# A planner that credits VectorE for TensorE's side products, and other costs in its ledger, in a two-layer decoder step

## The chip, the core and the metric

One NeuronCore of a Trainium2 chip runs the whole program. The metric is the time of one execution on the device, in microseconds; the comparison is between medians of repeated runs. Five engines matter: TensorE (PE in the profile; PEld is its loading of stationary operands), VectorE (DVE), ScalarE (ACT), GpSimd (POOL) and SyncE (SP), whose queue issues most of the transfers. Each runs its own instructions in the order in which the program gives them, and waits for the others by semaphores.

## What is computed

One inference step of a decoder with two layers, for 256 prompt tokens and 8 sequences of 4 tokens (288 columns in all), width 1024, in float32. In each layer four token mixers run beside each other on one input projection, and their outputs are merged through sigmoid gates:

```python
g_cols, u_pool, u_conf, u_sc, q, k, v, qi, ki, wi = split_cols(x @ w_in)
a_out, new_pool = pool_mixer(u_pool, ...)
cv, new_conf = causal_dwconv(ga * jax.nn.sigmoid(gb), st_conf, conv_w)       # 31 taps, 256 channels
b_out = jax.nn.silu(layer_norm(cv + conv_b, conv_ln_g, conv_ln_b))
c_out = sb * cc                                                              # short convolution, 3 taps
d_out = attend(q, k, v, qi, ki, wi)                                          # top-k by indexer scores, then softmax
merged = gates[0]*(a_out @ w_br_pool) + gates[1]*(b_out @ w_br_conv) + gates[2]*(c_out @ w_br_sconv) + gates[3]*(d_out @ w_br_attn)
x1 = layer_norm(ALPHA * x + merged @ w_o, ln1_g, ln1_b)
r = ALPHA * x1 + (silu(hg) * hu) @ w_ffn_out
r = r + (pe @ w_pe) * jax.nn.sigmoid(r @ w_pg)
y = layer_norm(r, ln2_g, ln2_b)
```

## The kernel before

**Weights.** All weights are 128x128 tiles, 2448 of them, in groups of eight (`G`). A group is loaded by one transfer on SP's queue (`load`, L252), ScalarE rounds it to its high half (`high`, L260, tile `whi`), and VectorE makes the low half as the difference (`low`, L267, tile `wlo`). Inputs are split in the same way, and `mm3` (L289) multiplies each tile three times, high by high, high by low and low by high, in three matmuls of 288 columns (L292 to L294; L318 to L324 where several outputs grow together). A group is thus 24 matmuls. `fetch` (L237) issues transfers five groups ahead of the matmuls, high halves three and low halves two ahead; `wlo` has three buffers.

**Order.** The order is written out by the program, engine by engine, and a planner fills it. `W` (L277) is called for each tile; at the first tile of a group it calls `fetch` and then `side` (L205). `side` is one tick of the planner: it raises `left`, what remains of VectorE's and ScalarE's time in this group, by `budget` = (1.96, 2.3) us, with no surplus carried over but debts kept, and then steps the tasks that are awake, as long as `left` is above zero for the engines that a task needs. A task is a generator; it issues instructions and yields their cost (VectorE, ScalarE), or a number of ticks to sleep. So what a task issues in a tick stands, on every engine, behind the weight halves that `fetch` has just issued and ahead of the group's 24 matmuls; that holds for the tasks' own TensorE work too (the "products": index scores, attention scores, transposes, convolution statistics). Work outside the tasks, the evacuation of projections, is issued behind its group and takes its cost off with `cost` (L219). `finish` (L223) steps tasks to their end without ticks of weight work between.

**Tasks.** In each layer `layer` (L1110) starts the 31-tap convolution `conv` (L670) at the lowest rank, `index_prompt` (L756), `index_sample` (L928), `attn_prompt` (L801), `attn_sample` (L970), `sconv` (L568) and `pool` (L603). They run beside the projections: q, k, v with rotary, short convolution, pool, gates 0 and 2, branches 0 and 2, gates 1 and 3. Then the attention tasks are finished, branch 3 runs, the convolution is finished, and w_o with branch 1 begins. A convolution step is one `scalar_tensor_tensor` on 128x256 (L684, planned at 0.49).

**Banks.** Projections rotate through four PSUM banks (`mm`), products through four (`ax`, `get_ax`). A projection of 8 row blocks fills one bank in a group. A branch (`branch`, L1067) of `nk` = 2 row blocks fills four in a group; VectorE multiplies each by its gate (L1075 for the first branch; L1078, then an addition on GpSimd at L1079), and 0.37 is charged behind each.

**Last norm.** `ln` (L386) ends by `first` (VectorE multiplies by the inverse deviation, L439) and `second` (scale and shift). In the last norm (`not after`) ScalarE does `second` (L446) for all channel blocks but 3 and 7, which VectorE does (L448); six transfers of the output (L453) follow on SP.

## Time and profile before

| | us |
|---|---|
| median of three runs | 1073.88 (1073.39 to 1074.95) |
| the profiled execution | 1073.4 |
| its span on the core | 1071.5 |
| TensorE's matmuls busy | 1055.5 |
| VectorE busy | 763.2 |
| ScalarE busy | 564.2 |
| GpSimd busy | 157.1 |

The span is from the first to the last instruction of the program; 1.9 us of the profiled execution's time lie around it. A matmul's record is longer than the distance to the next matmul, since matmuls are pipelined: whether TensorE loses time is read from the distance between starts and from its idle time, not from busy time alone. Layer 0's mixers lie at about 28 to 245 us, layer 1's at about 557 to 777; between and behind them are w_o, feed-forward, gate projection and norms. `[idle <-X]` behind an instruction says how long its engine stood idle before it, and what ended that.

### The profile page before, as it was taken

What the parts mean: (1) busy time and instruction counts of PE and PEld (TensorE: products, weight loads), DVE (VectorE), ACT (ScalarE), POOL (GpSimd) and SP (SyncE); (2) the same over time, 40 slices, a digit from 0 to 9 for tenths busy, and PEclk for the clock granted to TensorE, in tenths of its full rate; (3) what the DMA queues carried; (4) which work ended last, traced back from release to release, by engine and by line L of the source; (5) the groups of instructions that cost most, each with busy time, mean ns of one, the idle gap of its engine ahead of it and who ended that gap; (6) DMA issues with size and microseconds to landing.
All of it is one profiled execution on the core that took longest, in us unless ns stands there. A gap on an engine that the chain in (4) does not pass through costs nothing.

```text
span 1071.5 us, 20583 instructions
## 1 busy us (share of the span) xinstructions
PE 1055.5 (98%) x8078; PEld 1022.4 (95%) x8078; DVE 763.2 (71%) x1319; ACT 564.2 (53%) x950; POOL 157.1 (15%) x177
## 2 busy tenths in 40 slices
PE   9999999999999999999999999999999999999996
PEld 8999989899999999999999999898999999999996
DVE  5898869668785565544789888786688756555456
ACT  4886446554564444434578665554645644443344
POOL 0530003005500000000425100030055000000004
PEclk9999999999999999999999999999999999999998
DMA  8577646554455555544555766465453545554541
GB/s 304 168 247 213 201 144 227 197 167 147 150 164 172 157 171 168 174 157 169 161 183 164 264 190 216 122 225 205 139 169 128 186 158 170 171 171 159 171 143 45
DMA packets 61778, 188.57 MB, mean 176 GB/s; under 512 B 7602, under 2 KB 12274, under 8 KB 61682
## 3 DMA queue, kind: packets, MB, share of 16 engines
q1 hardware_dynamic: 60546, 183.55, 52.8%
q0 software_dynamic: 992, 3.57, 1.0%
q8 instruction: 63, 1.03, 0.4%
q14 instruction: 33, 0.27, 0.1%
q10 hardware_dynamic: 144, 0.15, 0.1%
HBM read 182.49 MB, written 4.75 MB: 175 GB/s over the span
## 4 chain that ended last, share of the span: by engine, by line
PE 90%; DVE 4%; ACT 2%; issue 1%; DMA 1%; POOL 1%; SPq 1%; POOLq 0%; DVEq 0%; ACTq 0%
PE mm L292 25%; PE mm L293 25%; PE mm L294 24%; PE mm L322 2%; PE mm L324 2%; PE mm L318 2%; DVE wlo L271 1%; DMA wraw<-in_w_dram 1%; POOL b L374 1%; PE ax L293 1%; PE ax L294 1%; PE ax L292 1%; DVE b L684 1%; PE ax L993 1%; PE ax L1030 1%
## 5 line engine op out<-in xcount | busy, mean ns | idle before, releaser
L271 DVE TENSOR_TENSOR wlo<-wraw,whi 128x1024 fp32r<-128x1024 f32 (+1 forms) x309 | 385.7, 1251 | 161.6 <-issue 80.8
L292 PE MATMUL mm<-xh,whi 128*128 128x288 f32 x1536 | 455.5, 297 | 1.0 <-DVE s L1078 1.0
L293 PE MATMUL mm<-xl,whi 128*128 128x288 f32 x1536 | 453.1, 295 | 0.0
L294 PE MATMUL mm<-xh,wlo 128*128 128x288 f32 x1536 | 452.9, 295 | 0.2 <-DVE wlo L271 0.2
L264 ACT ACTIVATE whi<-wraw 128x1024 fp32r<-128x1024 f32 (+1 forms) x309 | 322.7, 1047 | 160.8 <-PE mm L293 80.7
L292 PEld LDWEIGHTS mm<-xh,whi 128*128 128x128 f32 x1536 | 288.8, 188 | 9.3 <-issue 7.3
L294 PEld LDWEIGHTS mm<-xh,wlo 128*128 128x128 f32 x1536 | 288.6, 188 | 0.6 <-DVE wlo L271 0.6
L293 PEld LDWEIGHTS mm<-xl,whi 128*128 128x128 f32 x1536 | 288.8, 188 | 0.3
L292 PE MATMUL mm<-b,whi 128*128 128x288 f32 x576 | 171.5, 298 | 1.9 <-DVE m L1075 1.9
L293 PE MATMUL mm<-b,whi 128*128 128x288 f32 x576 | 169.9, 295 | 0.0
L294 PE MATMUL mm<-b,wlo 128*128 128x288 f32 x576 | 169.5, 294 | 0.0
L292 PEld LDWEIGHTS mm<-b,whi 128*128 128x128 f32 x576 | 107.9, 187 | 2.8 <-DVE m L1075 2.6
L294 PEld LDWEIGHTS mm<-b,wlo 128*128 128x128 f32 x576 | 108.5, 188 | 0.0
L293 PEld LDWEIGHTS mm<-b,whi 128*128 128x128 f32 x576 | 108.1, 188 | 0.2
L1079 POOL TENSOR_TENSOR m<-m,s 128x288 f32<-128x288 f32 x32 | 37.7, 1209 | 268.5 <-DVE s L1078 268.5
L343 POOL TENSOR_TENSOR b<-xf 128x288 f32<-128x288 f32 x4 | 4.9, 1215 | 443.0 <-DVE xf L1230 434.4
L1203 ACT ACTIVATE b<-s 128x288 fp32r<-128x288 f32 x44 | 19.2, 444 | 92.3 <-DVE s L1198 92.3
L684 DVE SCALAR_TENSOR_TENSOR b<-b,prm 128x256 f32<-128x256 f32 x120 | 58.9, 539 | 0.1
L1198 DVE TENSOR_TENSOR s<-s,mm 128x288 f32<-128x288 f32 x40 | 18.0, 454 | 50.6 <-PE mm L294 50.6
L1063 ACT ACTIVATE xf<-mm 128x288 f32<-128x288 f32 x32 | 13.2, 411 | 53.9 <-PE mm L294 53.8
L1063 ACT ACTIVATE g<-mm 128x288 f32<-128x288 f32 x32 | 13.2, 411 | 47.9 <-PE mm L294 47.8
L1206 DVE TENSOR_TENSOR b<-s,b 128x288 fp32r<-128x288 f32 x44 | 19.8, 457 | 19.4 <-ACT b L1203 19.4
(252 smaller groups left out, 1198.2 us busy)
## 6 DMA issues: line engine op xcount, KB each, us to landing
wraw<-in_w_dram SPq DMA_DIRECT2D x304, 512.0 KB, 3.5
kv<-in_ck_dram SPq DMA_DIRECT2D x32, 260.0 KB, 5.3
kv<-in_cv_dram SPq DMA_DIRECT2D x32, 256.0 KB, 5.2
out_ko_dram<-b POOLq DMA_DIRECT2D x2, 576.0 KB, 3.4
out_vo_dram<-b POOLq DMA_DIRECT2D x2, 576.0 KB, 5.8
kv<-in_kidx_dram SPq DMA_DIRECT2D x32, 32.0 KB, 2.8
b<-in_p_dram SPq DMA_DIRECT2D x3, 288.0 KB, 3.8
wraw<-in_w_dram SPq DMA_DIRECT2D x3, 256.0 KB, 5.3
```

What stands on the lines that cost most here:

```text
L264: self.nc.scalar.activation(self.hi[g][:, c[i]], self.raw[g][:, c[i]], AF.Copy)
L271: self.nc.vector.tensor_tensor(self.lo[g][:, c[i]], self.raw[g][:, c[i]], self.hi[g][:, c[i]].bitcast(F32), op=OP.subtract)
L292: m(out, wh, rh, start=first, stop=False)
L293: m(out, wh, rl, start=False, stop=False)
L294: m(out, wl, rh, start=False, stop=last)
L318: m(o, wh, rh[:, k], start=k == 0, stop=False)
L322: m(o, wh, rl[:, k], start=False, stop=not early and k == nk - 1)
L324: m(o, wl, rh[:, k], start=False, stop=False)
L684: nc.vector.scalar_tensor_tensor(o, e, wj, o, op0=OP.mult, op1=OP.add)
L1063: self.nc.scalar.activation(g, a, AF.Sigmoid)
L1079: nc.gpsimd.tensor_tensor(self.m[:, j], self.m[:, j], t, op=OP.add)
L1206: nc.vector.tensor_tensor(h[:, 1, i % 2], t, h[:, 0, i % 2].bitcast(F32), op=OP.subtract)
```

## The change

- `budget` for ScalarE is 2.1 instead of 2.3; a gate is charged 0.41 instead of 0.3; the exponentials of `attn_prompt` are issued only in a tick where ScalarE has 1.6 left.
- A new `gain` adds 0.8 of a product's time to what is left of VectorE's budget, at the places where products are issued.
- Three sleeps of one tick become two, ahead of the convolution's mean, the normalised transposes and the sample's index product, and one of two becomes three, ahead of the prompt's index products.
- The convolution's mean and variance are one matmul each, of a sum that VectorE makes first, instead of two; the two squares are made by VectorE instead of ScalarE.
- `branch` charges 0.46 for an evacuation instead of 0.37, and those of the first group before its first tile; each evacuation later charges for one of the group to come.
- In the last norm GpSimd scales block 6 and ScalarE block 3.

```diff
@@ -129,7 +129,7 @@
-        self.budget = (1.96, 2.3)
+        self.budget = (1.96, 2.1)
@@ -219,6 +219,10 @@
         self.left[1] -= a
+
+    def gain(self, t):
+
+        self.left[0] += 0.8 * t
@@ -442,7 +446,9 @@
             y = ys.pop(k)
-            if not after and k not in (3, 7):
+            if not after and k == 6:
+                nc.gpsimd.tensor_scalar(xf[:, k], y, g[:, k:k + 1], b[:, k:k + 1], op0=OP.mult, op1=OP.add)
+            elif not after and k < KD - 1:
                 nc.scalar.activation(xf[:, k], y, AF.Identity, bias=b[:, k:k + 1], scale=g[:, k:k + 1])
@@ -694,24 +700,29 @@
             nc.vector.tensor_scalar(cv[:, c, TP:], cv[:, c, TP:], bias[:, c:c + 1], None, op0=OP.add)
             yield 0.1, 0
+        both = self.s()
+        nc.vector.tensor_tensor(both, cv[:, 0], cv[:, 1], op=OP.add)
+        yield 0.45, 0
         yield BOTH
         self.free()
         self.free()
-        yield 1
+        yield 2
         mu, var = yield from self.get_ax(2)
         mu, var = mu[:, :N], var[:, :N]
-        for c in range(2):
-            nc.tensor.matmul(mu, self.c("o1024"), cv[:, c], start=c == 0, stop=c == 1)
+        nc.tensor.matmul(mu, self.c("o1024"), both, start=True, stop=True)
+        self.gain(0.25)
         sq = [self.s(), self.s()]
         for c in range(2):
             nc.vector.scalar_tensor_tensor(cv[:, c], mu, -4.0, cv[:, c], op0=OP.mult, op1=OP.add)
             yield 0.4, 0
         for c in range(2):
-            nc.scalar.activation(sq[c], cv[:, c], AF.Square)
-        yield 0, 0.8
+            nc.vector.tensor_tensor(sq[c], cv[:, c], cv[:, c], op=OP.mult)
+            yield 0.45, 0
+        nc.vector.tensor_tensor(sq[0], sq[0], sq[1], op=OP.add)
+        yield 0.45, 0
         yield 1
-        for c in range(2):
-            nc.tensor.matmul(var, self.c("o1024"), sq[c], start=c == 0, stop=c == 1)
+        nc.tensor.matmul(var, self.c("o1024"), sq[0], start=True, stop=True)
+        self.gain(0.25)
         sd = self.s()
         nc.scalar.activation(sd, var, AF.Sqrt, bias=self.c("eps"), scale=4.0)
         yield 0, 2.0
@@ -758,7 +769,7 @@
         yield 0, 0.33
-        yield 2
+        yield 3
         wp = self.sb.tile([128, 2, 4], F32, name="wp", tag="wp", bufs=1)
@@ -776,6 +787,7 @@
                                  start=True, stop=True)
+            self.gain(0.4 + n / 400)
             for e in range(2):
@@ -833,6 +846,7 @@
                                      self.k[r, h // 2, :n], start=True, stop=True)
+                self.gain(1.1)
@@ -846,6 +860,8 @@
             yield 1
+            while self.left[1] < 1.6:
+                yield 1
             for h in range(8):
@@ -857,7 +873,7 @@
                 yield 0.06 + n / 1920, 0
-            yield 1
+            yield 2
             pts = []
@@ -881,6 +898,7 @@
                                          pts[kc][:, 2 * c + s], start=kc == 0, stop=kc == i)
+            self.gain(1.0 * (i + 1))
             self.free(len(pts))
@@ -939,12 +957,13 @@
             yield 0, 0.22
-        yield 1
+        yield 2
         a = yield from self.get_ax()
         for p in range(4):
             nc.tensor.matmul(a[32 * p:32 * p + 32, :NK], self.qibd[:, p].rearrange("p r h t -> p (r h t)"),
                              self.kx[:, p], start=True, stop=True)
         nc.tensor.matmul(a[:, 288:288 + NS], self.c("hsel")[:4], self.wi[:, TP:], start=True, stop=True)
+        self.gain(1.2)
         rl = self.sb.tile([128, NK], F32, name="rls", tag="rls", bufs=1)
@@ -993,6 +1013,7 @@
                                      kt[j][:, :, c], start=False, stop=c == 3)
+            self.gain(2.3)
@@ -1029,6 +1050,7 @@
                                      start=False, stop=kc == 1)
+            self.gain(3.0)
@@ -1061,16 +1084,19 @@
             g = self.xf[:, j] if spare else self.sb.tile([128, N], F32, name="g", tag="g", bufs=9)
             self.nc.scalar.activation(g, a, AF.Sigmoid)
-            self.cost(0, 0.3)
+            self.cost(0, 0.41)
             self.gates[i, j] = g
 
     def branch(self, i, name, nk, first=False):
         nc = self.nc
         h, l = self.br.pop(name)
+        now = G // nk
+        self.cost(0.46 * now, 0)
         for j in range(KD):
             a, = self.proj("w_br_" + name, [128 * j], h, l, nk)
             g = self.gates.pop((i, j))
-            self.cost(0.37, 0)
+            if j + now < KD:
+                self.cost(0.46, 0)
             if first:
...
```

Further calls of `gain`, each behind its product: 0.4 behind a transposition of v, 0.35 behind four transposes of the probabilities and of the sample's output, 0.6 behind the sample's index sum.

## Rows read from the trace of the kernel before

**Rows 1.** Page of the profile, parts 1 and 4: busy time; last chain by engine.

```profile
PE 1055.5 (98%) x8078; PEld 1022.4 (95%) x8078; DVE 763.2 (71%) x1319; ACT 564.2 (53%) x950; POOL 157.1 (15%) x177
...
PE 90%; DVE 4%; ACT 2%; issue 1%; DMA 1%; POOL 1%; SPq 1%; POOLq 0%; DVEq 0%; ACTq 0%
```

**Rows 2.** Windows view: stretch; us, busy us (instructions) by engine, clock, DMA share, GB/s.

```profile
44.00:77.00 33.00, 33.00 (x252) 32.29 (x251) 31.27 (x67) 27.46 (x57) 12.31 (x15) 1.00 0.67 213
```

**Rows 3.** Timeline, TensorE, 38 to 46: start, us, line, operation, tiles, count, [idle <-releaser].

```profile
41.65 0.29 PE L294 MATMUL mm<-xh,wlo 128*128 128x288 f32 x1
...
43.61 0.71 PE L777 MATMUL ax<-ki,qi 64*128 64x128 f32 x6 [1.03 <-ACT ki L759]
44.25 0.40 PE L292 MATMUL mm<-xh,whi 128*128 128x288 f32 x1
```

**Rows 4.** Timeline, VectorE, 162 to 180, layer 0's branches.

```profile
163.57 1.23 DVE L271 TENSOR_TENSOR wlo<-wraw,whi 128x1024 fp32r<-128x1024 f32 x1 [0.30 <-issue]
164.71 1.67 DVE L684 SCALAR_TENSOR_TENSOR b<-b,prm 128x256 f32<-128x256 f32 x4
166.41 1.55 DVE L1075 TENSOR_TENSOR m<-mm,xf 128x288 f32<-128x288 f32 x4
...
174.22 1.73 DVE L271 TENSOR_TENSOR wlo<-wraw,whi 128x1024 fp32r<-128x1024 f32 x1
...
176.83 1.54 DVE L1078 TENSOR_TENSOR s<-mm,g 128x288 f32<-128x288 f32 x4
```

**Rows 5.** Waits, 160 to 180: who waited for whom, us, times, longest.

```profile
PE mm L292 <- DVE s L1078: 0.6, 1, 0.6
...
PE mm L292 <- DVE m L1075: 0.3, 1, 0.3
```

**Rows 6.** Waits, 690 to 712, layer 1's branches.

```profile
PE mm L292 <- DVE m L1075: 1.7, 2, 0.9
...
PE mm L292 <- DVE s L1078: 0.3, 1, 0.3
```

**Rows 7.** Timeline, ScalarE, 688 to 712.

```profile
691.72 1.28 ACT L851 ACT_TABLE_LOAD   x1
...
698.37 0.41 ACT L1063 ACTIVATE g<-mm 128x288 f32<-128x288 f32 x1
```

**Rows 8.** Chain that ended last, in order of time: start, us, what.

```profile
222.64 0.97 PE ax L704 x4
226.79 0.97 PE ax L714 x4
```

**Rows 9.** Groups by line, VectorE, shapes apart: busy us, mean ns | idle before.

```profile
L736 DVE TENSOR_TENSOR b<-b,s 128x288 f32<-128x288 f32 x4 | 1.6, 452 | 0.0
```

**Rows 10.** Timeline, TensorE, 573 to 574.6, the same products in layer 1.

```profile
573.16 0.29 PE L294 MATMUL mm<-xh,wlo 128*128 128x288 f32 x1
...
574.25 0.40 PE L292 MATMUL mm<-xh,whi 128*128 128x288 f32 x1
```

**Rows 11.** Timeline, VectorE, 690 to 712.

```profile
699.76 1.23 DVE L271 TENSOR_TENSOR wlo<-wraw,whi 128x1024 fp32r<-128x1024 f32 x1 [1.39 <-ACT whi L264]
```

**Rows 12.** Windows view of instructions on the ax banks alone.

```profile
77.00:162.00 85.00, 14.43 (x130) 8.06 (x130) 6.62 (x14) 6.40 (x16) 1.00 0.61 196
```

**Rows 13.** Windows view, all instructions.

```profile
77.00:162.00 85.00, 85.00 (x663) 78.38 (x663) 68.73 (x157) 45.95 (x93) 1.50 (x3) 1.00 0.61 196
```

**Rows 14.** Timeline, GpSimd, 1057 to 1072.

```profile
1062.69 3.80 POOL L434 TENSOR_TENSOR xf<-xf,b 128x288 f32<-128x288 f32 x5 [2.34 <-ACT b L419]
```

**Rows 15.** Timeline, SP's queue, 1057 to 1072.

```profile
1065.29 3.76 SPq L453 DMA_DIRECT2D out_y_dram<-xf  x6
```

**Rows 16.** Timeline, VectorE, 1057 to 1072.

```profile
1065.98 0.67 DVE L448 TENSOR_SCALAR xf<-s,prm 128x288 f32<-128x288 f32 x1
...
1067.78 0.43 DVE L448 TENSOR_SCALAR xf<-s,prm 128x288 f32<-128x288 f32 x1
```

**Rows 17.** Timeline, VectorE, 28 to 46.

```profile
35.24 1.97 DVE L684 SCALAR_TENSOR_TENSOR b<-b,prm 128x256 f32<-128x256 f32 x2
```

More of the change, by code (lines that the diff above doesn't have):

```diff
@@ L811, in attn_prompt @@
                 nc.tensor.transpose(a[:rows, 128 * c:128 * (c + 1)], self.v[:, c, 128 * i:128 * i + rows], ident)
+            self.gain(0.4)
             nc.scalar.activation(vt[:, i] if i < 2 else vs, a[:rows], AF.Copy)
@@ L871, in attn_prompt @@
                                                              128 * kc:128 * (kc + 1)], ident)
+                    self.gain(0.35)
                     nc.scalar.activation(pt[:, h0:h0 + 4], v, AF.Copy)
@@ L957, in index_sample @@
         nc.tensor.matmul(a[:NS, :NK], ws, rl, start=True, stop=True)
+        self.gain(0.6)
         sc = self.sb.tile([NS, NK], F32, name="scs", tag="scs", bufs=1)
@@ L1040, in attn_sample @@
             self.free()
+            self.gain(0.35)
             w = slice(TP + 16 * f, TP + 16 * f + 16)
```

## The prediction

> **What bounds the kernel now.** I read the page's shares first: TensorE's matmuls are busy for 1055.5 of 1071.5 us, and the chain that ended last lies on TensorE for 90% of the span [rows 1]. So there are two ways to gain: less work on TensorE, or fewer of the 16 us in which it stands still. VectorE and ScalarE cost nothing by being busy; they cost where TensorE waits for them. I therefore went along TensorE's timeline and the chain of waits, looking for gaps between one weight matmul and the next. In the stretch 44 to 77 us 252 matmuls take 33.00 us [rows 2], a step of 0.13 us. Against that step three kinds of gap stand in the stages that the change touches: a product in layer 0 that waits for its operand [rows 3], evacuations that come late where branches follow each other [rows 4 to 7], and the products themselves, which are work and stay. The part between the layers' attention stages (feed-forward, layer norms) is not touched but for the last norm.
>
> **The change part by part.**
>
> *Two products become one, in four places.* The convolution's mean and variance take two matmuls each; the pair takes 0.97 us of the chain, for the mean as for the variance [rows 8], so one takes 0.485. Two pairs in each of two layers: 4 x 0.485 = **1.94 us** off TensorE. In their place VectorE gets, per layer, one sum ahead of the mean, two squares (from ScalarE) and one sum of squares: four operations of the kind that takes 0.45 [rows 9], 1.8 us. This lies at the end of the convolution, a chain that nobody awaits until after the fourth branch, so I cost it at nothing. If that cover is gone, it is because the variance product, which still stands one group behind its operand, comes up before five VectorE operations in a row are through (2.3 us behind the mean, of a group's 3.2); then the whole group of weight matmuls queues behind it on TensorE, and the square root waits for it. That is up to 0.5 us in each layer, and stands in the term for new waits.
>
> *The index product one group later.* In layer 0 the key copy on ScalarE comes late and the first index products stand 1.03 us idle for it: from the last weight matmul before them to the first one behind them go 41.65 to 44.25, 2.60 us [rows 3]. The same products in layer 1 take 573.16 to 574.25, 1.09 us [rows 10]. The difference, 1.51 us, is wait. A group is 24 matmuls, 3.2 us, so one group more removes the wait. What is late next is VectorE: in 44 to 77 it is busy for 31.27 of 33.00 us [rows 2], 1.73 us free, and the change gives it there 0.8 x (0.72 + 1.04) = 1.4 us of budget (the two credits of the index products, worked out from the code). TensorE would arrive 1.5 us sooner at an engine with no more room than that; only the low halves that were made ahead give a little. Bounds 0.3 and 1.5; I take **0.9 us**. The other products that move by a group (transposes, sample index, convolution) show no such idle time, so they gain nothing; the attention chain gets up to three groups longer by them, and the page loads that it issues on SP between the weight loads move along, at no cost as long as the chain ends within the last gates.
>
> *The branches.* A branch of two row blocks has four outputs in a group and four banks, so an output's evacuation must be through within one group. Before, the cost (0.37) is taken off only behind each output: the planner fills the first group with convolution steps and then finds that it is short. One sees this at 163.57: low half, four convolution steps (1.67), and only at 166.41 the first evacuation [rows 4]; again at 174.22 with a step between low half and evacuation at 176.83. TensorE stands idle 0.3 + 0.6 us in layer 0 [rows 5] and 1.7 + 0.3 us in layer 1 [rows 6], 2.9 in five gaps. The records overlap: a matmul lasts 0.29, or 0.40 right behind a gap, but the step is 0.13 [rows 2 and 3], so each gap loses 0.27 more than its idle time: 2.9 + 5 x 0.27 = 4.2 us. After, 4 x 0.46 = 1.84 stands against the budget of 1.96 ahead of the first group, and no convolution step fits: the evacuation begins at 164.8, the end of the low half, not 166.41, and the 0.5 us gap is gone; behind 174.22 the removed step moves the evacuation from 176.83 to 175.95. In layer 0 I count 1.2 of its 1.4 us. In layer 1 part of the wait isn't VectorE's own: ScalarE runs the table load and eight exponentials from 691.72 on, the gate behind them comes only at 698.37 [rows 7], and so the low half at 699.76 waits 1.39 us for its high half [rows 11], the next evacuations behind it in VectorE's queue. If the exponentials stay there, TensorE, 1.2 us sooner, waits longer at that point; if the added groups push them on by one or two, they lie behind the last gate and the wait goes. Of 2.8 us I count 1.8. Together **3.0 us**, bounds 1.0 and 4.2.
>
> *The credit of four fifths.* In 77 to 162 us products and the index projection keep TensorE busy for 14.43 us on ax banks [rows 12], so VectorE gets up to 0.8 x 14.4 = 11.5 us more in a stretch where it is busy for 68.73 of 85.00 [rows 13]. It fits: 80.3 of 85. But it only brings the convolution forward, which is at the lowest rank and which no one awaits. Cost and gain: nothing. It takes from the lead that VectorE has on TensorE, and a product that still stands one group behind a VectorE operand could feel it: new waits of 0 to 3 us; I take **0.6**, nearer to nothing, because 4.7 us stay free.
> The Trainium skill (Perfetto Trace Analysis, Optimizing Scalar/DVE Operations) says that with VectorE saturated, work may well be moved from it to ScalarE; the change goes the other way. The trace agrees in 44 to 77 and has VectorE at 81% in 77 to 162; by that rule the result is the third rival below.
>
> *ScalarE's budget* (2.3 to 2.1, a gate 0.41 for 0.3, exponentials only with 1.6 left) hands out less work to an engine that TensorE waits for in one place; alone nothing, its delay is in the term for the branches.
>
> *The last norm.* Channel block 6 goes from ScalarE to GpSimd, block 3 from VectorE to ScalarE. GpSimd's queue is through at about 1066.5; an operation there takes 3.80 / 5 = 0.8 us [rows 14]. Block 6 would be ready at about 1067.7; ScalarE has six in a row as before. Six output transfers are issued one behind the other on SP from 1065.29 to 1069.05 [rows 15], and the last three follow block 5 on ScalarE, which hardly moves: **+0.1 us**, bounds -0.2 and +0.5.
> VectorE's scaling of a block lasts 0.67 while GpSimd runs and 0.43 when it doesn't [rows 16]: beside each other they slow down by half. The Trainium skill (SBUF — State Buffer, SBUF: two separate sides) says that the port pair of the two is an exclusive lock and the loser blocks for the whole instruction; by that, block 7 would wait for all of block 6, and the term would be +0.4. The sum would be 0.3 us higher.
>
> Sum against the profiled execution's 1073.4 us: -1.94 - 0.9 - 3.0 + 0.6 + 0.1 = -5.1, 1068.3 us. The median of the runs lies 0.5 above the profiled one; I say **1068.5**.
>
> **The rivals.**
> 1. *The waits only move.* The exponentials stay ahead of the branches and VectorE's lack of room eats the index wait: -1.94 - 0.3 - 0.5 + 0.6 + 0.1 = -2.0, 1071.4 to 1072. For it: the 1.39 us behind ScalarE [rows 11], and 95% in 44 to 77 [rows 2]. Against it: in layer 0 the step ahead of the evacuation is plain, and the advance charge removes just that.
> 2. *All waits go.* Bounds at their best, no new ones: -1.94 - 1.5 - 4.2 = -7.6, 1065.8.
> 3. *VectorE becomes the bound (slower).* Where GpSimd runs, a convolution step takes 0.99 (1.97 for two) [rows 17] and not 1.67 / 4 = 0.42. If the credited steps cost double, 11.5 us become 23, 6.7 more than the 16.3 free in 77 to 162, and 1.4 become 2.8, 1.1 more than are free in 44 to 77; less 3.2 us for one of the two groups by which low halves are made ahead, 4.6 us in each layer, 9.2 in all, in place of the 0.6 for new waits: 1068.3 + 8.6 = 1076.9. It decides at 16.3 / 11.5 = 1.4 us of VectorE per credited us. Against it: GpSimd is busy for 1.50 us in those 85 [rows 13].
> 4. *The change does not do what it says:* the credit, its headline, moves no end. I hold this for true; it is in the forecast.
>
> **How the numbers follow.** Forecast (1066.3 to 1071) 0.60, waits only move 0.17, all go 0.12, VectorE bound 0.11. A measurement tells some 0.2% from no change, 2.15 us: faster is below 1071.7, slower above 1076.0. Faster: 0.60 less 0.03 for its upper edge, 0.12, and half of 0.17: 0.77. Slower: 0.07 of the 0.11. Same: 0.16. The range leaves out the slower rival and a little of the others: 1065.4 to 1072.8.
>
> **What would show it.** Right: the two products of the convolution at 0.49 each; no idle time for the key copy in layer 0; in the branches evacuations right behind the low half, with no idle TensorE for them; the convolution's mean product several groups sooner than 222.6. Wrong: low halves that TensorE waits for in 44 to 110 (rival 3), the long wait for a high half again in layer 1 (rival 1). The forecast also fails if the attention tasks end behind the last gates: the rest of them would then be issued with no weight matmuls between, several us in each layer.

## The result, and the profile after

The changed kernel takes **1088.59 us** (median, 1087.39 to 1091.96), the kernel before, timed beside it, 1073.64 us (1071.89 to 1074.95): a ratio of 1.0146, interval 1.0124 to 1.0167. The forecast was 1068.5, and the time lies far above the range. The profiled execution took 1087.39 us with a span of 1085.6, 14.1 us more than the span before.

Two lines of the page of the changed kernel, its busy times and its last chain by engine:

```profile
PE 1061.7 (98%) x8070; PEld 1024.9 (94%) x8070; DVE 763.9 (70%) x1326; ACT 560.3 (52%) x945; POOL 156.8 (14%) x178
...
PE 66%; DVE 6%; ACT 3%; issue 1%; POOL 1%; DMA 0%; ACTq 0%; DVEq 0%; POOLq 0%
```

VectorE and ScalarE are as busy as before [rows 1], so the time was not lost to more work of theirs. The second line cannot be held against the 90% of [rows 1]: its shares add up to 77%, since the trace follows the chain back only to 246.98 us, the end of the hole described next, and no further.

To find the places, take the distance from each weight matmul to the next, less the usual step of 0.131 us, and add it up by stage (counting what is over 0.05 us). Between 28 and 275 us (layer 0's mixers and branches) this sum is 42.69 us, and was 34.14; in layer 1's (560 to 800) it is 38.00, and was 33.30; in all other stages together it differs by 0.4, and the end of the program by 0.4. The sum holds products as well as waits, so what it gained is waiting or slower matmuls. One place in each layer accounts for more than all of it: between the last gate's group and the first group of the fourth branch. Layer 0, the timeline of TensorE (start, us, line, operation, tiles, count, idle time ahead and what ended it):

```profile
235.22 0.29 PE L298 MATMUL mm<-xh,wlo 128*128 128x288 f32 x1
237.99 0.69 PE L1039 MATMUL ax<-const,rls 128*128 128x128 f32 x2 [2.48 <-ACT rls L1025]
...
239.51 2.07 PE L1048 MATMUL ax<-vs,pst 32*128 32x512 f32 x2 [0.62 <-ACT pst L1043]
241.51 3.42 PE L1051 MATMUL ax<-kv,pst 128*32 128x512 f32 x16
245.83 0.66 PE L1061 MATMUL ax<-const,b 128*128 128x128 f32 x4 [0.90 <-ACT b L1055]
247.02 0.40 PE L296 MATMUL mm<-b,whi 128*128 128x288 f32 x1 [0.54 <-ACT b L1072]
```

From the last weight matmul at 235.22 to the next at 247.02 there are five kinds of products and no weight: the probabilities of the sample attention's second half transposed (L1039, and L1040, left out here), multiplied with the values (L1048, L1051), and transposed back (L1061). Four waits for ScalarE stand among them, 2.48 + 0.62 + 0.90 + 0.54 = 4.5 us; a table load of 1.28 us on ScalarE is part of the first. This is `finish`: the attention of the sample had not ended when the fourth branch needed it, so the rest of its steps was issued one behind the other. In the kernel before these products cost 3.6 us, spread over groups 53 to 55, with weight matmuls between them and no wait. Two lines of the kernel before, for L1048 and L1051 of the rows above:

```profile
206.34 1.12 PE L1027 MATMUL ax<-vs,pst 32*128 32x512 f32 x2
207.39 1.92 PE L1030 MATMUL ax<-kv,pst 128*32 128x512 f32 x16
```

In the changed kernel the distance is 11.67 us over the usual step: the same products are slower in the hole (2.07 and 3.42 us against 1.12 and 1.92), and behind it the weight matmuls are slower too. The windows view (stretch; us, busy us and instructions by engine, granted clock, DMA share, GB/s):

```profile
228.00:235.00 7.00, 7.00 (x66) 6.40 (x59) 2.93 (x7) 2.22 (x6) 0.00 (x0) 1.00 0.79 250
235.00:246.50 11.50, 7.49 (x29) 2.20 (x28) 1.45 (x6) 4.13 (x9) 0.00 (x0) 0.70 0.40 150
246.50:252.00 5.50, 4.88 (x23) 4.67 (x24) 2.79 (x5) 2.07 (x4) 0.80 (x1) 0.69 0.24 68
```

The clock granted to TensorE is 1.00 ahead of the hole, 0.70 in it and 0.69 in the 5.5 us behind it, where it is at the lower of its two levels, 1.2 GHz, for a part of the time. The hole and the slow group behind it come to 13.7 us in layer 0 and 9.5 in layer 1; less the 3.6 us of products, that is 10.1 + 5.9 = **16.0 us**.

What the prediction had counted on is there too. The index products of layer 0 stand without a wait (45.60 - 44.52 = 1.08, against 2.60 in [rows 3]):

```profile
44.52 0.29 PE L298 MATMUL mm<-xh,wlo 128*128 128x288 f32 x1
...
44.96 0.72 PE L788 MATMUL ax<-ki,qi 64*128 64x128 f32 x8
45.60 0.40 PE L296 MATMUL mm<-xh,whi 128*128 128x288 f32 x1
```

The convolution's mean product stands at group 56 instead of 58, two groups sooner. And in the branches the evacuations stand right behind the low half, with no convolution step between (VectorE, layer 0; compare [rows 4]):

```profile
160.45 1.22 DVE L275 TENSOR_TENSOR wlo<-wraw,whi 128x1024 fp32r<-128x1024 f32 x1
161.58 1.71 DVE L1101 TENSOR_TENSOR m<-mm,xf 128x288 f32<-128x288 f32 x4
```

A third kind of loss I had excluded: late weights. In layer 0 TensorE waits 2.7 us around 92 to 95 us, in layer 1 1.2 us at 633. These rows of the changed kernel show where it comes from. The waits of SP's queue, its timeline, the windows, and the first high half and low half behind:

```profile
SPq L933 <- PE ax L963: 9.8, 1, 9.8
```

```profile
74.09 12.65 SPq L933 DMA_DIRECT2D kv<-in_ck_dram  x5
86.85 8.63 SPq L261 DMA_DIRECT2D wraw<-in_w_dram  x5
```

```profile
74.00:80.00 6.00, 6.00 (x54) 5.61 (x53) 5.69 (x13) 3.73 (x10) 0.00 (x0) 1.00 0.93 309
80.00:86.00 6.00, 6.00 (x50) 5.38 (x48) 5.76 (x17) 1.64 (x6) 0.00 (x0) 1.00 0.03 10
```

```profile
92.81 1.06 ACT L268 ACTIVATE whi<-wraw 128x1024 fp32r<-128x1024 f32 x1 [10.47 <-DMA wraw<-in_w_dram]
```

```profile
93.90 1.22 DVE L275 TENSOR_TENSOR wlo<-wraw,whi 128x1024 fp32r<-128x1024 f32 x1 [4.96 <-ACT whi L268]
```

The sample's key pages (`ck`) and its index keys (`kidx`) share one set of four buffers (`kv`). The pages of the fourth sequence cannot be loaded before the index product (L963) has read its keys. That product now stands in group 23 instead of 21, so the page load waits 9.8 us for it, and SP's queue stands: the share of the DMA engines falls from 0.93 to 0.03 (in the kernel before it is 0.91 from 80 to 86 us), and the weight loads behind come after 86.85. ScalarE then waits 10.47 us for a weight, VectorE 4.96 us for ScalarE, and TensorE for both. In layer 1 the wait is 11.0 us. In the kernel before it is 3.7 us in layer 0 and costs nothing:

```profile
SPq L915 <- PE ax L945: 3.7, 1, 3.7
```

One group later is not yet too late: in the kernel before with one tick added (below) SP waits 8.1 us for this product, in group 22, and TensorE shows no such gap.

So the two stages lost 16.0 + 3.9 us at these places, and by the sums they lost 8.6 + 4.7 = 13.3 in all: everything else in them gained 6.6 us, where the forecast had counted on 1.94 + 0.9 + 3.0 = 5.8.

### The profile page after: what moved, and what is told of

It is laid out like the page before. It is cut to its first block, busy times and chain, and to the rows that moved or that the text cites. A ratio compares the mean times of both kernels' runs of the same rounds, so it can differ in the third digit from the quotient of the medians.

```text
span 1085.6 us, 20564 instructions
## 1 busy us (share of the span) xinstructions
PE 1061.7 (98%) x8070; PEld 1024.9 (94%) x8070; DVE 763.9 (70%) x1326; ACT 560.3 (52%) x945; POOL 156.8 (14%) x178
## 4 chain that ended last, share of the span: by engine, by line
PE 66%; DVE 6%; ACT 3%; issue 1%; POOL 1%; DMA 0%; ACTq 0%; DVEq 0%; POOLq 0%
PE mm L297 18%; PE mm L296 18%; PE mm L298 18%; DVE wlo L275 2%; PE mm L326 2%; PE mm L328 2%; PE mm L322 2%; PE ax L297 1%; PE ax L296 1%; PE ax L298 1%; ACT whi L268 1%; DVE m L759 1%; PE ax L326 1%; PE ax L328 1%; PE ax L322 1%
## 5 line engine op out<-in xcount | busy, mean ns | idle before, releaser
L296 PEld LDWEIGHTS mm<-b,whi 128*128 128x128 f32 x576 | 109.4, 190 | 1.7 <-ACT b L1072 1.6
L297 PEld LDWEIGHTS mm<-b,whi 128*128 128x128 f32 x576 | 109.5, 190 | 0.8 <-DVE b L1076 0.6
```

Source lines behind the costliest of these rows:

```text
L296: m(out, wh, rh, start=first, stop=False)
L297: m(out, wh, rl, start=False, stop=False)
```

## The experiments

The two theories that were told apart: **A**, the loss is the rest of the attention chain, issued in the open because the chain came late; **B**, the third rival of the prediction, VectorE has become the bound through the credit, and the holes follow from it. Then the parts alone, to price the terms of the sum, and the parts taken away again from a version that works.

How late the chain is can be read from the trace: count the groups of 24 weight matmuls that have gone ahead of the two score products of the sample's attention (its two halves). The fourth branch begins with group 63 in layer 0 and 217 in layer 1; behind its second score product the chain needs six or seven groups more. "Hole" is the distance at the fourth branch over the usual step.

| kernel | halves, layer 0 | halves, layer 1 | holes, us | median, us | ratio to before (interval) |
|---|---|---|---|---|---|
| before | 34, 49 | 187, 205 | none | 1073.1 to 1073.6 | |
| changed | 41, 61 | 194, 214 | 11.67, 7.51 | 1088.59 | 1.0146 (1.0124 to 1.0167) |
| before, second half delayed | 34, 61 | 187, 214 | 11.93, 8.92 | 1089.88 | 1.0155 (1.0139 to 1.0172) |
| before, one tick | 40, 56 | 194, 212 | 0, 5.15 | 1074.80 | 1.0022 (1.0010 to 1.0033) |
| changed, two numbers back | 34, 51 | 187, 205 | none | 1069.08 | 0.9967 (0.9955 to 0.9980) |
| changed, no credit | 41, 61 | 195, 215 | 10.82, 11.28 | 1097.33 | 1.0233 (1.0216 to 1.0250) |
| changed, only the tick back | 41, 61 | 194, 213 | 11.47, 6.16 | 1081.20 | 1.0087 (1.0065 to 1.0109) |

### The late second half alone

```diff
                 kt = yield from self.load_pages("ck", f)
-                yield 2
+                yield 15 if self.l == 0 else 12
```

> The kernel before, with nothing changed but the sleep ahead of the second half of the sample's attention: 15 ticks in layer 0 and 12 in layer 1 instead of 2, so that what is left of it at the last gates is the same as in the changed kernel (from the load of the value pages and the exponential on in layer 0, from the scaling by the own keys on in layer 1). Theory A (the loss is the rest of the attention chain, issued with no weight matmuls between): the hole of 11.67 us in layer 0 and of 7.51 us in layer 1 of the changed kernel appear here, each less 3.9 us of products that were work before too, each with some 2 us of slower matmuls behind it: 10 + 6 = 16, so 1086 to 1091 us. Theory B (the credit made VectorE the bound, and the holes are a by-thing of it): there is no credit here, so 1073 to 1076 us.

Measured: 1089.88 us, holes of 11.93 and 8.92 us. The windows of layer 0, in the same stretches as above:

```profile
235.00:246.50 11.50, 8.43 (x38) 3.35 (x36) 1.91 (x8) 3.22 (x7) 0.00 (x0) 0.75 0.57 202
246.50:252.00 5.50, 4.15 (x15) 3.55 (x16) 2.34 (x4) 2.75 (x5) 0.00 (x0) 0.50 0.00 0
```

The same hole in a kernel that has nothing of the change costs 16.8 us (1089.88 less 1073.06), near the 16.0 counted for the holes of the changed kernel, the lower clock behind it (0.50) included. That is what theory A expected. B falls as the cause of this loss: there is no credit in this kernel.

### One tick in the kernel before

```diff
             yield 0, 0.22
-        yield 1
+        yield 2
         a = yield from self.get_ax()
```

> The kernel before with one sleep changed: the sample's index product stands two ticks behind its operands instead of one, as in the changed kernel. Theory A (one tick puts the index of the sample behind the eight exponentials of the prompt in ScalarE's budget, and the chain never catches up): the sample's top-k starts about six groups later in both layers, and what is left at the last gates is the final two subtractions in layer 0 (0 to 1 us) and all from the copy of the second output on in layer 1 (3 to 5 us): 1076 to 1079 us. Theory B (VectorE's credit): one tick of sleep costs at most one group of a chain that nobody awaits, 1073 to 1074.5 us.

Measured: 1074.80 us, ratio 1.0022. One tick of sleep moves the sample's score product from group 34 to 40 and from 187 to 194, as in the changed kernel, and leaves a hole in layer 1:

```profile
767.16 0.29 PE L294 MATMUL mm<-xh,wlo 128*128 128x288 f32 x1
767.38 1.12 PE L1027 MATMUL ax<-vs,pst 32*128 32x512 f32 x2
768.43 1.92 PE L1030 MATMUL ax<-kv,pst 128*32 128x512 f32 x16
771.24 0.66 PE L1039 MATMUL ax<-const,b 128*128 128x128 f32 x4 [0.89 <-ACT b L1033]
772.44 0.40 PE L292 MATMUL mm<-b,whi 128*128 128x288 f32 x1 [0.54 <-ACT b L1049]
```

From 767.16 to 772.44 there are 5.28 us, of which 3.4 are products that were work before. So the mechanism is as theory A says, the lag of six groups included, but the kernel is 1.7 us slower and not 3 to 6: only the transposition at the end still waits in the open. Why one tick becomes six groups can be worked out from the code. A task needs both budgets above zero, except in the top-k, which asks for VectorE's alone (`yield VECTOR`). In the kernel before, the sample's index has its second product and the first step of its top-k behind it in group 24; in group 25 `attn_prompt` issues its eight exponentials, 5.81 us in the planner's cost against 2.3 a tick, and ScalarE's budget stays below zero for three ticks. All other tasks stand in these, and the top-k has VectorE to itself, four or five steps in a tick: it is through by group 30. One tick later, the second product falls into the tick of the exponentials, and the top-k can't begin: it waits out the debt as the others do, and then shares VectorE with them, two steps in a tick, until group 37. The exponentials were a lane for whoever was already in the top-k.

### The changed kernel with two numbers put back

```diff
-        self.budget = (1.96, 2.1)
+        self.budget = (1.96, 2.3)
...
             yield 0, 0.22
-        yield 2
+        yield 1
         a = yield from self.get_ax()
```

> The changed kernel with two numbers put back: the sample's index product one tick behind its operands, and ScalarE's budget at 2.3. Everything else of the change stays, the credit and the advance charge too. Theory A: the chain ends four groups ahead of the fourth branch in both layers, both holes are gone, and the gains of the prediction stand: 1.9 (convolution) + 1.5 (index wait) + 3 to 4 (branches) below 1073.6, less up to 4 us of the small waits that the changed kernel shows elsewhere: 1066 to 1070 us. Theory B: the credit is still there, so the time stays above 1080 us.

Measured: 1069.08 us, ratio 0.9967 (0.9955 to 0.9980), no hole. With these two numbers, everything else of the change stands and the kernel is 4.0 us faster than before, close to the forecast. B falls: the credit is there. SP's wait for the index product is short again, 2.5 us.

One wait of the first rival remains. In layer 1 the exponentials still stand ahead of the first branch; ScalarE's and VectorE's timelines (the exponentials left out but for the last):

```profile
687.93 1.28 ACT L867 ACT_TABLE_LOAD   x1
...
692.69 0.50 ACT L867 ACTIVATE b<-b,st 128x256 f32<-128x256 f32 x1
...
693.30 1.28 ACT L1086 ACT_TABLE_LOAD   x1
694.59 0.41 ACT L1086 ACTIVATE g<-mm 128x288 f32<-128x288 f32 x1
694.90 2.94 ACT L268 ACTIVATE whi<-wraw 128x1024 fp32r<-128x1024 f32 x3
```

```profile
695.98 1.23 DVE L275 TENSOR_TENSOR wlo<-wraw,whi 128x1024 fp32r<-128x1024 f32 x1 [2.60 <-ACT whi L268]
```

Between the exponentials and the next high half stand a table load and a gate's sigmoid; the low half waits 2.60 us for its high half, the evacuations stand behind it in VectorE's queue, and TensorE waits 1.5 us for them.

### The changed kernel without the credit

```diff
     def gain(self, t):
 
-        self.left[0] += 0.8 * t
+        self.left[0] += 0.0 * t
```

> The changed kernel with the credit at nothing instead of 0.8; all else stays. Theory A: the chain is as late as before in layer 0 and a little later in layer 1, and the convolution is late as well, so both holes stay: 1086 to 1093 us. Theory B (the credit is the cause): the time falls to 1070 or below.

Measured: 1097.33 us, slower than the changed kernel by 8.7. B predicted the other sign. The holes stay (10.82 and 11.28), and more than I expected comes on top: the convolution, at the lowest rank and now without credit, isn't ready when its branch begins, at 801 to 804 us in layer 1, where TensorE waits 1.5 us for ScalarE and 0.5 for VectorE. The advance charge and the added VectorE steps take from VectorE's budget; without the credit nothing pays for them.

### Only the tick put back

```diff
             yield 0, 0.22
-        yield 2
+        yield 1
         a = yield from self.get_ax()
```

This is the version with two numbers put back, with ScalarE's budget at 2.1 again.

> The changed kernel with one number put back, the sample's index product one tick behind its operands; against the kernel with two numbers put back it differs by ScalarE's budget alone, 2.1 instead of 2.3. The prediction's step for the budget: it costs nothing, 1069 us. Theory A: with 0.2 less a group the sample's index product comes after the exponentials again, six groups later; the sample's attention is at its value pages at the last gates in layer 0 and at its transposes in layer 1, and the holes come back, some 10 and 5 us: 1082 to 1087 us.

Measured: 1081.20 us, a little under the 1082 to 1087 expected; holes of 11.47 and 6.16 us, as expected in size, while the slow group behind layer 1's is missing. The budget alone is worth 12 us here. Tick and budget are two ways over the same edge: in the kernel before the tick suffices to make the chain late, and in the changed one, with its longer sleeps and charges, the budget does. The changed kernel with the tick but the old budget was not run.

### The parts alone

The convolution: one matmul each for mean and variance, sums and squares on VectorE, no sleep changed.

```diff
-        for c in range(2):
-            nc.tensor.matmul(mu, self.c("o1024"), cv[:, c], start=c == 0, stop=c == 1)
+        nc.tensor.matmul(mu, self.c("o1024"), both, start=True, stop=True)
...
-        for c in range(2):
-            nc.tensor.matmul(var, self.c("o1024"), sq[c], start=c == 0, stop=c == 1)
+        nc.tensor.matmul(var, self.c("o1024"), sq[0], start=True, stop=True)
```

> The kernel before with the convolution's part alone: its mean and variance are one matmul each, of a sum made on VectorE, and VectorE makes the squares; no sleep is changed. By the prediction's step: four times 0.485 us less on TensorE, nothing for VectorE's four added operations: 1.9 us below the kernel before, 1071.1. Rival: the variance product, one group behind five VectorE operations, waits for them, up to 0.5 us in each layer: 0.9 us below.

Measured: 1071.23 against 1073.10 us, ratio 0.9986 (0.9977 to 0.9995): 1.9 us, as worked out.

The charge for the branches alone.

```diff
+        now = G // nk
+        self.cost(0.46 * now, 0)
         for j in range(KD):
             a, = self.proj("w_br_" + name, [128 * j], h, l, nk)
             g = self.gates.pop((i, j))
-            self.cost(0.37, 0)
+            if j + now < KD:
+                self.cost(0.46, 0)
```

> The kernel before with the charge for the branches alone (0.46 for an evacuation, those of the first group ahead of it). Theory of the prediction: the stalls in the branches go, 1.2 of 1.4 us in layer 0 and 1.8 of 2.8 in layer 1, together 3.0 us below the kernel before, 1070.1. Rival (seen in the kernel with two numbers put back): in layer 1 the eight exponentials stay one group ahead of the first branch, and the late high half behind them takes back most of the 2.8 us there: 1.5 to 2.2 us below, 1071 to 1071.5.

Measured: 1074.99 against 1073.10 us, ratio 1.0018 (1.0009 to 1.0026): slower, where I forecast 3 us faster and the rival some 2. In layer 0 the branch stalls are gone. But while the branches hold VectorE's budget below zero, the prompt's tasks stand, and behind them they go in a burst. In layer 1, VectorE's eight scalings of the probabilities, and TensorE's transposes of them, one group behind:

```profile
711.24 3.33 DVE L858 TENSOR_SCALAR b<-b,st 128x256 f32<-128x256 f32 x8
```

```profile
713.32 2.52 PE L870 MATMUL ax<-const,b 128*128 128x128 f32 x15 [1.23 <-DVE b L858]
```

TensorE stands 1.23 us for the scalings, and the distance over the usual step is 3.77 us where these sixteen transposes take 1.67 without a wait; together with the wait behind the exponentials, which stays, layer 1 loses 1.7 us, where it should have gained. The scalings are slow besides: 3.33 us for eight, the first of them while GpSimd runs the branch's additions; without additions, in layer 0, they take 2.19 (the last rows of this document). In layer 0 of the profiled execution the sum of the distances grows by 1.1 us: 0.5 at the same transposes and a stretch at a lower clock (below) take back more than the branches gain. That execution, 1076.73 us, is the slowest of the twelve; how many of the others had the slow stretch is not shown.

The credit alone.

```diff
+    def gain(self, t):
+
+        self.left[0] += 0.8 * t
```

and its calls behind the products.

> The kernel before with the credit alone: 0.8 of each product's time is added to VectorE's budget. Theory A (the credit moves nothing that anyone awaits): the convolution ends six groups sooner, the sample's attention one to three groups later and still four groups ahead of the fourth branch; within 1 us of the kernel before, 1072 to 1074. Theory B (VectorE has no room for the credited steps): low halves come late in the groups with products, 1075 us or more.

Measured: 1078.40 us, ratio 1.0050 (1.0037 to 1.0063). Theory A's "within 1 us" fails, and so does my step that cost the credit at 0.6. But the place is not B's, the groups with products: it is the branches. The credit brings the prompt's exponentials two groups forward in layer 1, into the gates, and hands out convolution steps into the first group of the branch. ScalarE loads a table at 687.57, runs the eight exponentials, loads the next one at 692.93 and has three sigmoids and three high halves to catch up with. VectorE at the same time:

```profile
695.62 1.23 DVE L275 TENSOR_TENSOR wlo<-wraw,whi 128x1024 fp32r<-128x1024 f32 x1 [3.39 <-ACT whi L268]
696.76 1.67 DVE L688 SCALAR_TENSOR_TENSOR b<-b,prm 128x256 f32<-128x256 f32 x4
698.35 1.22 DVE L275 TENSOR_TENSOR wlo<-wraw,whi 128x1024 fp32r<-128x1024 f32 x1
699.48 1.67 DVE L688 SCALAR_TENSOR_TENSOR b<-b,prm 128x256 f32<-128x256 f32 x4
701.07 1.18 DVE L694 TENSOR_TENSOR b<-b,prm 128x992 f32<-128x992 f32 x1
702.17 1.54 DVE L1091 TENSOR_TENSOR m<-mm,xf 128x288 f32<-128x288 f32 x4
```

The low half at 695.62 waits for its high half (3.39 us, by the trace's idle time), then four convolution steps, a low half, four more and a 1.18 us step stand ahead of the first evacuation at 702.17; TensorE waits 3.4 us for it. Layer 0 has 1.80 and 0.94 us of the same. The convolution does end sooner, its mean product in group 52 instead of 58, as theory A had it.

### The parts taken away from the version that works

Each is the kernel with two numbers put back, at 1069.08 us (0.9967), with one part undone.

```diff
-            yield 2
+            yield 1
             pts = []
```

> The kernel with two numbers put back, and with the transposes of the probabilities one tick behind their operands instead of two. The prediction's step: no idle time stands ahead of these transposes in the kernel before, so the sleep gains nothing, 1069 us. Theory (from the kernel with the charge for the branches alone, where TensorE stands 1.23 us for the scaled probabilities in layer 1): the advance charge lets the tasks go in a burst behind the branches, VectorE makes the eight scalings late, and the transposes wait for them, 2.2 us in layer 1 and 0.5 in layer 0: 1071 to 1072 us.

Measured: 1076.34 us, ratio 1.0026 (1.0016 to 1.0035): 7 us lost by the medians and 6 by the ratios, where my step said nothing and the theory 2 to 3. TensorE's distances show both waits for the scalings, 2.5 us in layer 0 and 2.1 in layer 1, and a stall of 1.68 us in the branch of layer 0: without the sleep the prompt's second exponentials come one group earlier, ahead of the branch. Of the three parts taken away here it is the one that costs most.

The branches charged as before:

```diff
-        self.cost(0.46 * now, 0)
...
-            if j + now < KD:
-                self.cost(0.46, 0)
+            self.cost(0.37, 0)
```

> The kernel with two numbers put back, and with the branches charged as in the kernel before (0.37 behind each evacuation, nothing ahead). The prediction's step: 3.0 us of the branch stalls come back, 1072 us. Theory: with the credit, the convolution's steps stand ahead of the evacuations as in the kernel with the credit alone (stalls of 2.7 us in layer 0 and 4.3 in layer 1, against 0 and 1.7 here), so 5 us: 1074 us. Rival: without the charge the tasks run on evenly through the branches, and the other waits shrink by as much: 1069 to 1070 us.

Measured: 1070.53 us, ratio 0.9975 (0.9967 to 0.9984): 1.4 us by the medians, 0.9 by the ratios, and the interval overlaps that of 0.9967 (0.9955 to 0.9980), so a cost is not clear of noise; nearest to the rival. The branch stalls return (0.42, 0.40 and 0.39 in layer 0; 1.80 and 0.93 in layer 1 in place of 1.67), but 5 us was wrong. So the credit without the advance charge does not cost here what it costs alone: other parts of the change take most of that loss away, and which of them is not shown.

The prompt's index products two ticks behind:

```diff
         yield 0, 0.33
-        yield 3
+        yield 2
         wp = self.sb.tile([128, 2, 4], F32, name="wp", tag="wp", bufs=1)
```

> The kernel with two numbers put back, and with the prompt's index products two ticks behind the key copy instead of three. The prediction's step: 0.9 us lost, 1070 us. By the traces: the wait of 1.5 us comes back whole, 1070.6; and where the granted clock falls behind it, as in two of the kernels run (0.51 and 0.60 in the 3.5 us behind it, where the kernel before has 1.00), another 1.0 to 1.5 us: 1071.5 to 1072.

Measured: 1069.94 us, ratio 0.9968 (0.9956 to 0.9979), not to be told from 0.9967. The wait is in the trace (2.05 us in all against 0.95), the granted clock stays at 1.00 behind it, and the time doesn't show it: this sleep gains nothing here that can be measured. The planner moves other work with it: in layer 1 the prompt's second exponentials come two groups earlier, and the stall behind them is 1.25 us instead of 1.67, so the run doesn't price the wait alone.

### A version that beats both

The kernel with two numbers put back, and the exponentials held back while gates run.

```diff
-            while self.left[1] < 1.6:
+            while self.left[1] < 1.6 or self.gating:
                 yield 1
...
     def gate(self, i, spare=False):
+        self.gating = True
         for j in range(KD):
...
+        self.gating = False
```

> The changed kernel with two numbers put back (the sample's index product one tick behind, ScalarE's budget 2.3), and with the prompt's exponentials held back while gates are run. The planner moves them by one group in layer 1 alone, from the last gate's group into the first of the branch, and the attention chain still ends four groups ahead of the fourth branch. Theory: the table load and the sigmoid no longer stand between the exponentials and the next high half, so the stall of 1.67 us in the first branch of layer 1 goes: 1067 to 1068 us, 0.1 to 0.2% below the kernel with the two numbers put back. Rival: the high half comes as late behind the exponentials in the branch, and the stall only moves by a group: 1069 us.

Measured: **1066.35 us** against 1073.10, ratio 0.9938 (0.9925 to 0.9951). ScalarE in layer 1, with the exponentials one group later:

```profile
691.17 1.28 ACT L868 ACT_TABLE_LOAD   x1
...
695.93 0.50 ACT L868 ACTIVATE b<-b,st 128x256 f32<-128x256 f32 x1
...
696.42 1.99 ACT L269 ACTIVATE whi<-wraw 128x1024 fp32r<-128x1024 f32 x2
```

The high half follows the last exponential at once, with no table load and no sigmoid, and no stall is left in the branch. The stall did not move, it went. The kernel gains 2.7 us by the medians, 1 us more than the stall of 1.67; what the rest is the run doesn't show.

## Why the prediction was wrong, point by point

- **What bounds the kernel** was right: TensorE, less its waits.
- **The step that failed** stands in the part on the index product: "the attention chain gets up to three groups longer ... at no cost as long as the chain ends within the last gates". The condition was the whole question, and I did not work it out. I added sleeps (three ticks) where the chain's length is set by the planner: a task moves only while both budgets are above zero, so a tick lost in the wrong place costs the wait for ScalarE's debt. The chain came 12 groups later at its second half in layer 0 and 9 in layer 1, where 6 and 4 were to spare, and the holes that came of it cost 16.0 us. The last sentence of the prediction names the outcome, but no chance stood behind it: the slower case rested on the third rival alone.
- **ScalarE's budget, "alone nothing"**, was wrong by 12 us with the rest of the change in and the sample's sleep at one tick: 1081.20 against 1069.08.
- **The page loads, which "move along, at no cost"**, were wrong: SP's queue stood 9.8 us in layer 0 and 11.0 in layer 1 for the delayed index product, some 3.9 us of TensorE's time in both layers. I had looked at what is issued, not at what the issue waits for.
- **The convolution's products**, 1.94: measured 1.9.
- **The index wait**, 0.9 of 1.5 taken: the wait goes, but nothing of it can be told from the time; the doubt about VectorE's room was right, the term too large.
- **The branches**, 3.0: right in layer 0 by the trace, and in layer 1 of the version with two numbers put back the first rival had the place (the low half's wait of 2.60 us behind the exponentials); there the charge is worth 0.9 to 1.4, not clear of noise, and alone it costs 1.9. The term was priced as if the tasks that it pushes out came back for nothing.
- **The credit** at 0.6: alone it costs 5.3, through the branches and not through the third rival's groups; in the changed kernel taking it away costs 8.7. Neither is a property of the credit: what it does depends on what the rest of the ledger charges and delays.
- **The transposes' sleep** was cost at nothing since no wait stood ahead of them; the other edits make the waits that it covers, 7 us. An edit that covers a wait which only the rest of the change makes can't be priced from the trace of before alone.
- **The last norm**, +0.1. In the version with two numbers put back, the outputs are issued on SP from 3.09 to 6.99 us behind the start of the norm's last products, and in the kernel before from 2.29 to 6.05 (from 1065.29 [rows 15]; the products start at 1063.00 there). 0.80 of this is the products themselves, 1.91 us for the eight against 1.11, at a granted clock of 0.53 against 1.00; without it the end is 0.14 later, near the term. Its rows (TensorE, SP, GpSimd, VectorE):

```profile
1057.92 1.91 PE L430 MATMUL ax<-q,const 128*128 128x72 f32 x8 [0.96 <-DVE q L425]
...
1061.01 3.90 SPq L459 DMA_DIRECT2D out_y_dram<-xf  x6
1062.62 0.58 POOL L450 TENSOR_SCALAR xf<-s,prm 128x288 f32<-128x288 f32 x1 [1.22 <-DVE s L443]
1062.91 0.45 DVE L454 TENSOR_SCALAR xf<-s,prm 128x288 f32<-128x288 f32 x1
```

GpSimd's scaling took 0.58 us, VectorE's beside it 0.45, against 0.43 alone [rows 16]. The Trainium skill (SBUF — State Buffer, SBUF: two separate sides) calls the port pair of the two an exclusive lock, by which I had weighed +0.4 here; the Trainium skill there also limits the lock to some of VectorE's operations. These rows show no block: VectorE's scaling began 0.29 us behind GpSimd's and ran beside it.
- **The sum.** Two numbers away from the change, the kernel takes 1069.08 us, and the forecast was 1068.5. That is luck more than a sum that was right: of its terms the convolution's alone was measured at its size, the charge for the branches and the credit each make the kernel before slower, and the transposes' sleep, which stood at nothing, hides 6 to 7 us. The gate's charge, the wait for 1.6 left, the convolution's longer sleep and the last norm were not run by themselves. What decided the changed kernel was whether the chain ends in time, and the sum had no term for it.

## What to carry to other kernels

Where a planner fills a static order, price an edit of its costs or sleeps by when the last dependent chain ends, not by the work that it moves: find the chain with the least slack, and the first point where it must pass another task for a shared budget. A change of one tick can cost six groups there. And of every instruction that is moved, ask who waits for the buffer that it frees: a transfer on an in-order queue may be the one, with all weights behind it.

## What the runs showed of the hardware

**The clock.** Where TensorE stands for the key copy in layer 0 (2.46 us between weight matmuls, with the products), the granted clock behind it was 1.00 in the kernel before and 0.51 in the kernel with the branches' charge alone; 44.5 to 48 us of both:

```profile
44.50:48.00 3.50, 3.50 (x28) 3.50 (x28) 3.00 (x5) 3.40 (x7) 1.66 (x2) 1.00 0.63 211
```

```profile
44.50:48.00 3.50, 3.50 (x16) 3.50 (x17) 3.01 (x6) 3.27 (x7) 1.57 (x2) 0.51 0.58 195
```

16 matmuls instead of 28 run in these 3.5 us, near the lower of the two levels, 1.2 GHz: 1.5 us, behind the same gap, in one execution and not in the other. It is 0.60 in the kernel with the credit alone, and 1.00 in those with the convolution alone, with one tick and with the late second half. So a gap of this size cost as much again as its wait of 1.5 us in one of six executions, somewhat less in another, and nothing in four, and I had taken no such term.

**VectorE beside GpSimd.** Where GpSimd adds up a branch, VectorE's steps take longer. GpSimd and VectorE in layer 0 of the kernel with the branches' charge alone:

```profile
173.61 8.59 POOL L1082 TENSOR_TENSOR m<-m,s 128x288 f32<-128x288 f32 x8 [68.93 <-DVE s L1081]
```

```profile
179.55 3.33 DVE L684 SCALAR_TENSOR_TENSOR b<-b,prm 128x256 f32<-128x256 f32 x4
...
183.94 1.66 DVE L684 SCALAR_TENSOR_TENSOR b<-b,prm 128x256 f32<-128x256 f32 x4
...
186.88 2.19 DVE L858 TENSOR_SCALAR b<-b,st 128x256 f32<-128x256 f32 x8
```

Four convolution steps take 3.33 us, and 1.66 behind the additions, which end at 182.2. Taken one by one, the three that begin while additions run last 1.02 to 1.04 us each, the others 0.47. The eight scalings take 2.19 alone and 3.33 in layer 1, where additions run to 713.1: there two of them last 0.88 us, the others 0.34 to 0.41. GpSimd is slowed as well: the addition that begins at 178.44, beside a low half, takes 1.86 us, and others 0.81. The third rival's price (twice the time beside GpSimd, [rows 17]) is real, but it applies to the branches, where charges of 0.46 and 0.49 meet steps of 0.4 to 0.8.
